# A hybrid decoder layer on one core: one pair of the second FFN computed plainly, and ScalarE and VectorE instructions placed by hand where stages change

## The chip, the cores and the metric

The kernel runs on one core of a Trainium2 chip. The core's engines work in parallel, each on its own queue of instructions: TensorE (matmuls and transposes; PE in the profile, its weight loads PEld), VectorE (DVE), ScalarE (ACT), GpSimd (POOL) and SyncE (SP), which here only starts DMA transfers. TensorE writes its products to PSUM, a memory of eight banks; everything else lies in SBUF. The metric is the time of the core in microseconds, the median of three runs: 1430.41 us before the change.

## The reference

A layer of a decoder is applied to 512 prompt tokens and to 64 sample tokens (8 sequences of 8), 576 in all, of width 1024, in fp32:

```python
x = x + 1/2 * swiglu(rmsnorm(x), ffn1)          # D_FF = 2816
P = rmsnorm(x) @ w_in                            # one combined projection
A = attention over 3 groups, (window, dilation) = (128,1), (512,4), (2048,16),
    4 heads x 64, RMSNorm of q and k; groups merged by their softmax denominators
B = gated linear attention, 4 heads, key 128, value 256, forget gate of rank 16;
    per-head RMSNorm, times silu(r_gate)
m = sigmoid(ga) * (A @ w_a_out) + sigmoid(gb) * (B @ w_b_out)
x = x + m @ w_out
x = x + 1/2 * swiglu(rmsnorm(x), ffn2)
swiglu(h) = (silu(h @ w_gate) * (h @ w_up)) @ w_down
```

Sample tokens attend to caches as well. Outputs are both groups of tokens, the new caches and the new states of the linear attention.

## The kernel before

**Tiles.** Activations are kept transposed: features on the 128 partitions, tokens along the columns, in two halves of 288. To reach fp32 accuracy each operand is split in two parts of the type fp32r, a high part that ScalarE rounds (line 138) and a low part that VectorE subtracts (line 139); each product then is three matmuls (high x high, high x low, low x high). A plain *group* is one 128-wide block of output features for one half of the tokens: 8 blocks of the contraction x 3 = 24 matmuls into one PSUM bank (`feat_mm`, lines 191 to 193). RMSNorm's gain is folded into the operand, and its factor per token, `row`, is multiplied to the product when VectorE takes it out of PSUM, so a stage may start before `row` is known.

**The FFN** (`sublayer`) has eleven pairs of 256 gate and up columns, worked off in phases of three pairs and a tail of two. The first `FIRST[g]` pairs are done plainly (class `First`, 8 groups of 24 matmuls for a pair; tiles pg). All later gates and ups are `Unit`s: seven products of block sums replace eight (12 matmuls for each product; tiles pX, pY, pZ), and so are the downs of the phases. Units need normalised operands in seven combinations, the tile `hop`, which VectorE and ScalarE build (`normal`, in steps `upper`, `lower`, `lower2`, `lower3`) during the plain groups, once `row` is there. `evac` takes a plain group out of PSUM: the factor (lines 642, 646, 648) and the Silu of the gate (643). `evacuate` calls it for groups that are at least two old, and then builds the pair's `second_operands`, the input of the down units. Before: three plain pairs in FFN 1 (g = 1), two in FFN 2 (g = 3). In FFN 2 the pool of weight tiles is exchanged at the seventh plain group (`buffers`).

**Between the stages.** When the last block of x is updated, `updated` puts off the sums of squares by `wait` groups and the row factors (`rows_`: transposes, and copies at line 222) by one more, so that TensorE runs the next stage's groups meanwhile; wait is 3 at the end of FFN 1 and 1 ahead of FFN 2.

**The mixer** (`mixer`) goes on after four r-gate groups that stand in the caller: their `gate_out` (oT = product x row, line 996), the r-gate's third block, then `PromptAttention` (head groups 1 and 2, then head group 0 with `steps0`, which runs beside the other r-gate blocks), `sample_steps` beside the first projections of the linear attention, the Silu of the eight r-gate tiles oT (line 1026), and the `Recurrence`.

**What sets the order.** TensorE's order is the order in which the program emits its instructions. The queues of the other engines are ordered by a scheduler, by readiness and by place in the emission; `keep_in_program_order` binds an instruction behind the one emitted just before it on its engine. `Weave` interleaves by hand: `run(main, between)` spreads the steps `between` evenly over the groups `main`, `put_off(n, step)` runs a step n groups later, and `loaded` gives a group a load that is emitted one group ahead. An empty step (`rest`) only takes a place. DMAs for weights are on SP's queue.

Of the kernel before, what the change touches and what calls it, by code (L numbers as in the profile page):

```python
# [18 lines left out]
P = 128  # L19
D = 1024  # L20
KD = D // P
SEQ = 512
# [12 lines left out]
GDV = 256  # L35
WCOLS = 1024
PAIRS = 3
FIRST = {1: 3, 3: 2}
AHEAD_W = 4


# [57 lines left out]
def hybrid_step_kernel(  # L99
# [131 lines left out]
    def updated(xT, m, h, g, sacc, sq, seen, wait=1):  # L231

        s = HALVES[h]
        operand(xT, m, s, g)
        if h not in [i for _, i in seen]:
            S.activation(sacc[:, s], xT[:, m, s], AF.Square)
        else:
            S.activation(sq, xT[:, m, s], AF.Square)
            V.tensor_add(sacc[:, s], sacc[:, s], sq)
        seen.append((m, h))  # L240
        if len(seen) < 2 * KD:
            return

        def sums():
            n = 5
            pr = ps_bg("pssq")
            V.memset(pr[NS:, 4:5], 0.0)
            for i in range(n):
                tok = sacc[:, SEQ:T] if i == 4 else sacc[:, i * P:(i + 1) * P]
                PE.matmul(pr[:tok.shape[1], i:i + 1], tok, ones, start=True, stop=True)  # L250
            rstd_of(rtok[:, :n], pr[:, :n], rms[:, :n], D)

        def rows_():
            spread([(rtok[:, t:t + 1], t * P) for t in range(4)], 0, SEQ)
            spread([(rtok[:NS, 4:5], SEQ)], SEQ, T)
            E.scaled(0, 1)

        weave.put_off(wait, sums)
        weave.put_off(wait + 1, rows_)

    E.scaled = lambda *halves: None
    wst = weights(4, 6, 1)
# [184 lines left out]
    def out(m, h):  # L447
        pt = ps_bg("py")
        for c in range(3):
            t0 = h * HALF + c * NC  # L450
            PE.transpose(pt[:NC, c * P:(c + 1) * P], xT[:, m, t0:t0 + NC], ident)
        y = ys2[:, (m + h) % 2]
        S.copy(y, pt[:NC, :3 * P])
        c = slice(m * P, (m + 1) * P)
        q = SP
        nt = 2 + (h == 0)
        q.dma_start(y_prompt[0, h * HALF:h * HALF + nt * NC, c].rearrange("(a p) c -> p a c", p=NC),
                    y[:, :nt * P].rearrange("p (a c) -> p a c", a=nt))
        if h:
            q.dma_start(y_prompt[0, SEQ - 32:SEQ, c], y[:32, 2 * P:])  # L460
# [88 lines left out]
def sublayer(E, xT, g, wg, wu, wd, wpre, after, nxt=lambda m: None, late=False, buffers=None):  # L549
# [41 lines left out]
    def normal():  # L591

        places.append(st.enter_context(E.sb("hop", 1, "right")).tile([P, 4 * slot], F32R, name="hop"))
        n = {}

        def factor(name, k, t):
            kk, s = {"A11": (k, 0), "A12": (k + 4, 0), "A21": (k, 1), "A22": (k + 4, 1)}[name]
            s = HALVES[s]
            V.scalar_tensor_tensor(t, xT[:, kk, s], E.gain[g][:, kk:kk + 1], E.row[:, s], op0=ALU.mult, op1=ALU.mult)
            n[name, k] = t  # L600
            return t

        def upper(name, k):
            E.split(*hact(name, k), factor(name, k, small("up", 8)))

        def lower(k):
            a21, a22 = (factor(x, k, small("s", 5)) for x in ("A21", "A22"))
            n["S1", k], n["S2", k] = small("s", 5), small("s", 5)
            V.tensor_add(n["S1", k], a21, a22)
            V.tensor_sub(n["S2", k], n["S1", k], n["A11", k])  # L610
            E.split(*hact("S2", k), n["S2", k])

        def lower2(k):
            E.split(*hact("S1", k), n["S1", k])
            V.tensor_sub(n["A11", k], n["A11", k], n["A21", k])
            E.split(*hact("S3", k), n["A11", k])

        def lower3(k):
            V.tensor_sub(n["A12", k], n["A12", k], n["S2", k])
            E.split(*hact("S4", k), n["A12", k])  # L620
            E.split(*hact("A22", k), n["A22", k])
# [15 lines left out]
    def evac(mat, f, h):  # L637
        s, po = HALVES[h], ps.pop((mat, f, h))[:, :HALF]
        c = kept.setdefault(f // 2, {})
        if mat == 0:  # L640
            c[C[f % 2, h]] = t = small("sg", 7) if f < 4 else small("up", 8)
            V.tensor_mul(t, po, E.row[:, s])
            S.activation(t, t, AF.Silu)
        else:
            u = small("s", 5)
            V.scalar_tensor_tensor(u, po, 0.5, E.row[:, s], op0=ALU.mult, op1=ALU.mult)
            t = c[C[f % 2, h]]
            V.tensor_mul(t, u, t)
            got[f // 2] = got.get(f // 2, 0) + 1

    got = {}

    def evacuate(i):
        for x in list(waiting):
# [50 lines left out]
    def up(pair):  # L705
        c = {}

        def done(i, x):
# [6 lines left out]
            if i == 6:  # L715
                c[name] = small("up", 8)
                V.scalar_tensor_tensor(c[name], x, 0.5, sg[name], op0=ALU.mult, op1=ALU.mult)
                kept[pair] = c
                if pair not in tail:
                    second_operands(pair)  # L720
                elif pair == tail[-1]:
                    last_operands()
                return
# [6 lines left out]
    def down(phase, m):  # L730
        f0, n = 2 * phase[0], len(phase)
        v = dv[:, f0:f0 + 2 * n, m * P:(m + 2) * P].rearrange("p (q two) c -> p two q c", two=2)

        def done(i, x):
            mm, h = {0: (0, 0), 1: (0, 0), 2: (1, 0), 3: (1, 1), 4: (1, 1), 5: (1, 0), 6: (0, 1)}[i]
            o = xT[:, m + mm, HALVES[h]]
            V.tensor_add(o, o, x)
        return Unit(E, [v[:, 0], v[:, 1]], lambda name, q: gact(name, phase[q]), n, done)


# [33 lines left out]

    final = []

    units = [fn(pair) for pair in phases[0][FIRST[g]:] for fn in (gate, up)]
    for n, phase in enumerate(phases):
        then = phases[n + 1] if n + 1 < len(phases) else tail
        units.append(gate(then[0]))  # L780
        downs = [down(phase, m) for m in range(0, KD, 2)]
        rest = [up(then[0])] + [fn(pair) for pair in then[1:] for fn in (gate, up)]
        units += rest + downs if then is tail else downs + rest
    lasts = [Last(m) for m in range(0, KD, 2)]

# [32 lines left out]

    for i, (_, u, n) in enumerate(slots):
        ahead(i)  # L820
        u.products(n)
        weave.tick()
        if isinstance(u, Last) and u.m == 4 and n in (1, 3):
            nxt(n // 2)
        evacuate(i)
        normal_steps(len(first) - i)
        if not any(isinstance(x[1], Unit) for x in slots[i + 1:]):
            for x in final:
# [158 lines left out]
def mixer(E, mxs, bk, xpool, opening):  # L987
# [7 lines left out]
    E.oT = oT = [E.slot(E.slotsA, F32, f"oT{m}") for m in range(KD)]  # L995
    gate_out = lambda m, s, ps: E.V.tensor_mul(oT[m][:, s], ps, E.row[:, s])

    for x in opening:
        gate_out(*x)
    weave.run(feat_groups(E, C_RG, [2], gate_out))  # L1000
    xpool.close()
    bk.close()
    bk = E.banks(4)
# [9 lines left out]
    weave.run(at.proj(0), at.steps12())  # L1013
    weave.run(feat_groups(E, C_RG, range(3, 8), gate_out), at.steps0())
    weave.finish()
    pst.close()
    bk.close()
    bk = E.banks(3)
# [1 line left out]
    hst = ExitStack()  # L1020
    gl = Recurrence(E, hst)
    early = gl.proj(0) + gl.proj(1)
    weave.run([lambda: gl.low_rank(Qm.pool)] + early[:13], sample_steps(E, sst, Qm))
    sst.close()
    for m in range(KD):
        S.activation(oT[m], oT[m], AF.Silu)
    gl.open(mxs)
    weave.run(early[13:], [gl.decay(0)])
    weave.run(gl.proj(2), gl.steps(0))
# [19 lines left out]
class PromptAttention:  # L1049
# [189 lines left out]
    def steps0(self):  # L1239
# [40 lines left out]

        rest = lambda: None
        (s0, t0, o0), (s1, t1, o1), (s2, t2, o2), (s3, t3, o3) = (one(n) for n in range(4))
        return [s0, s1, s2, t0, s3, t1, o0, t2, o1, t3, o2, rest, o3, rest, rest]


def sample_steps(E, st, Qm):
# [91 lines left out]
    def both(*steps):  # L1378
        def g():
# [2 lines left out]
        return g  # L1382

    f0(0)
    return [rest, k0[0], k0[1], s0[0], k0[2], s0[1], k0[3], both(s0[2], lambda: f0(1)), s0[3], rest, t0, rest,
            both(v0, lambda: f1(0)), o0, rest, rest, rest, k1[0], k1[1], s1[0], k1[2], s1[1], k1[3],
            both(s1[2], lambda: f1(1)), s1[3], rest, t1, rest, v1, rest, o1]


class Recurrence:  # L1390
# [18 lines left out]

    def low_rank(self, pool):  # L1410

        E, PE, S = self.E, self.E.PE, self.E.S
# [5 lines left out]
        S.copy(w[:, :, 0:16], raw)  # L1418
        E.V.tensor_sub(w[:, :, 16:32], raw, E.f32(w[:, :, 0:16]))
# [4 lines left out]
        for s in range(2):  # L1424
            S.copy(E.aup[32 * s:32 * s + 32], up)
        E.V.tensor_sub(E.aup[64:96], up, E.f32(E.aup[0:32]))
        self.lr = lr = hp.tile([96, T], F32R, tag="lr", name="lr", bufs=1)
        for s in HALVES:
# [311 lines left out]
```

## Time and profile before

| | |
|---|---|
| median of 3 runs | 1430.41 us (1430.05 to 1431.69) |
| the profiled execution | 1430.53 us, of which the span of the trace is 1428.7 |
| mean granted clock of TensorE | 0.993 |
| plain and unit weight splits on ScalarE (line 138) | 348 of 128x512, mean 577 ns; 115 of 128x1024, mean 971 ns |
| the same on VectorE (line 139) | 348, mean 632 ns; 115, mean 1128 ns |
| DMA | 144.28 MB, mean 101 GB/s |

"Busy" is time in which an engine executes; shares are of the span. The table of waits tells for how long TensorE stood before an instruction and who released it: `PE pf L191 <- ACT wh L138: 3.9, 1, 3.9` is TensorE ahead of the matmul of line 191 into tile pf, released by ScalarE's write of wh in line 138; sum of the waits, their number, the longest. In the tables of stretches and of the timeline, `xN` is the number of instructions. The granted clock is 1.00 where TensorE runs at full speed.

### The profile page before, as it was taken

What the parts mean: (1) busy time and instruction counts of PE and PEld (TensorE: products, weight loads), DVE (VectorE), ACT (ScalarE), POOL (GpSimd) and SP (SyncE); (2) the same over time, 40 slices, a digit from 0 to 9 for tenths busy, and PEclk for the clock granted to TensorE, in tenths of its full rate; (3) what the DMA queues carried; (4) which work ended last, traced back from release to release, by engine and by line L of the source; (5) the groups of instructions that cost most, each with busy time, mean ns of one, the idle gap of its engine ahead of it and who ended that gap; (6) DMA issues with size and microseconds to landing.
All of it is one profiled execution on the core that took longest, in us unless ns stands there. A gap on an engine that the chain in (4) does not pass through costs nothing.

```text
span 1428.7 us, 27553 instructions
## 1 busy us (share of the span) xinstructions
PE 1395.4 (98%) x10892; PEld 1366.0 (96%) x10892; DVE 1054.5 (74%) x2318; ACT 714.2 (50%) x1458; POOL 66.6 (5%) x105
## 2 busy tenths in 40 slices
PE   7999999999989999999999999999998999999997
PEld 7999999999989999898999999999998999999997
DVE  5999999998855454643576756455479999999882
ACT  7554564665444454632556634223345556466542
POOL 1000000000122211000000000000000000000000
PEclk9999999999999999999999999999999999999999
DMA  7313323332433432366223333335231333333332
GB/s 186 97 37 103 104 86 108 89 104 78 133 100 106 129 114 81 81 180 190 60 80 105 106 99 100 88 90 162 68 89 46 92 100 97 97 104 89 89 104 67
DMA packets 180688, 144.28 MB, mean 101 GB/s; under 512 B 7466, under 2 KB 179168, under 8 KB 180560
## 3 DMA queue, kind: packets, MB, share of 16 engines
q1 hardware_dynamic: 179456, 139.98, 33.8%
q0 software_dynamic: 1104, 2.54, 0.5%
q8 instruction: 86, 1.41, 0.4%
q14 instruction: 42, 0.34, 0.1%
HBM read 128.72 MB, written 13.78 MB: 100 GB/s over the span
## 4 chain that ended last, share of the span: by engine, by line
PE 89%; DVE 5%; ACT 2%; DMA 2%; issue 1%; SPq 1%; POOL 0%; ACTq 0%; POOLq 0%; DVEq 0%
PE pX L545 8%; PE pX L544 8%; PE pX L543 7%; PE pY L544 4%; PE pY L545 4%; PE pY L543 4%; PE pf L191 4%; PE pf L193 4%; PE pf L192 3%; PE ptok L956 3%; PE ptok L958 3%; PE ptok L957 3%; PE pZ L544 2%; PE pZ L545 2%; PE pZ L543 2%; PE pg L193 2%
## 5 line engine op out<-in xcount | busy, mean ns | idle before, releaser
L138 ACT CAST w<-raw 128x512 fp32r<-128x512 f32 (+1 forms) x348 | 196.8, 577 | 132.0 <-PE pX L545 31.2
L139 DVE TENSOR_TENSOR w<-raw,w 128x512 fp32r<-128x512 f32 (+1 forms) x348 | 215.9, 632 | 19.0 <-ACT w L138 17.4
L138 ACT CAST wh<-raw 128x1024 fp32r<-128x1024 f32 (+2 forms) x115 | 110.7, 971 | 118.1 <-PE pf L192 39.1
L139 DVE TENSOR_TENSOR wl<-raw,wh 128x1024 fp32r<-128x1024 f32 (+2 forms) x115 | 128.9, 1128 | 50.2 <-ACT wh L138 49.7
L545 PE MATMUL pX<-hop,w 128*128 128x288 f32 x544 | 161.5, 297 | 3.8 <-DVE w L139 3.8
L543 PE MATMUL pX<-hop,w 128*128 128x288 f32 x544 | 160.5, 295 | 1.1 <-ACT w L138 0.8
L544 PE MATMUL pX<-hop,w 128*128 128x288 f32 x544 | 161.4, 297 | 0.0
L191 PE MATMUL pf<-h,wh 128*128 128x288 f32 x384 | 119.9, 312 | 3.9 <-ACT wh L138 3.9
L956 PE MATMUL ptok<-wl,h 128*128 128x256 f32 x416 | 120.0, 289 | 0.0
L958 PE MATMUL ptok<-wh,h 128*128 128x256 f32 x416 | 116.9, 281 | 0.0
L957 PE MATMUL ptok<-wh,h 128*128 128x256 f32 x416 | 116.8, 281 | 0.0
L193 PE MATMUL pf<-h,wl 128*128 128x288 f32 x384 | 115.3, 300 | 0.4 <-DVE wl L139 0.4
L192 PE MATMUL pf<-h,wh 128*128 128x288 f32 x384 | 115.2, 300 | 0.0
L545 PEld LDWEIGHTS pX<-hop,w 128*128 128x128 f32 x544 | 102.9, 189 | 4.7 <-DVE w L139 4.7
L543 PEld LDWEIGHTS pX<-hop,w 128*128 128x128 f32 x544 | 103.1, 190 | 1.6 <-ACT w L138 1.0
L544 PEld LDWEIGHTS pX<-hop,w 128*128 128x128 f32 x544 | 103.0, 189 | 0.0
L191 PE MATMUL pg<-h,wh 128*128 128x288 f32 x320 | 96.4, 301 | 2.6 <-ACT wh L138 2.0
L193 PE MATMUL pg<-h,wl 128*128 128x288 f32 x320 | 95.6, 299 | 1.3 <-DVE wl L139 1.3
L192 PE MATMUL pg<-h,wh 128*128 128x288 f32 x320 | 95.7, 299 | 0.0
L191 PEld LDWEIGHTS pf<-h,wh 128*128 128x128 f32 x384 | 74.4, 194 | 7.0 <-ACT wh L138 4.1
L544 PE MATMUL pY<-hop,w 128*128 128x288 f32 x272 | 80.4, 296 | 0.0
L545 PE MATMUL pY<-hop,w 128*128 128x288 f32 x272 | 80.3, 295 | 0.0
(428 smaller groups left out, 4257.6 us busy)
## 6 DMA issues: line engine op xcount, KB each, us to landing
raw<-in_w_in_dram SPq DMA_DIRECT2D x58, 512.0 KB, 3.9
raw<-in_ffn_gate_dram SPq DMA_DIRECT2D x45, 512.0 KB, 3.8
raw<-in_ffn_up_dram SPq DMA_DIRECT2D x44, 512.0 KB, 3.8
raw<-in_ffn_down_dram SPq DMA_DIRECT2D x48, 384.0 KB, 3.3
raw<-in_ffn_down_dram SPq DMA_DIRECT2D x8, 512.0 KB, 3.5
kv<-in_cache_swa_kv_dram SPq DMA_DIRECT2D x32, 128.0 KB, 4.2
kv<-in_cache_swa_kv_dram SPq DMA_DIRECT2D x16, 256.0 KB, 4.4
S<-in_state_gla_dram SPq DMA_DIRECT2D x4, 1024.0 KB, 6.6
```

The costliest lines, as they stand in the source:

```text
L138: S.copy(hi, src)
L139: V.tensor_sub(lo, src, f32(hi))
L191: PE.matmul(ps, h, ah, start=first and j == 0, stop=False)
L192: PE.matmul(ps, h, al, start=False, stop=False)
L193: PE.matmul(ps, l, ah, start=False, stop=last and j == n - 1)
L543: PE.matmul(ps, wh[:, k], ah, start=opens and k == 0, stop=False, skip_group_check=True)
L544: PE.matmul(ps, wh[:, k], al, start=False, stop=False, skip_group_check=True)
L545: PE.matmul(ps, wl[:, k], ah, start=False, stop=k == self.nk - 1, skip_group_check=True)
L956: PE.matmul(po[:, :256], ah, wl, start=(k == 0), stop=False)
L957: PE.matmul(po[:, :256], al, wh, start=False, stop=False)
L958: PE.matmul(po[:, :256], ah, wh, start=False, stop=(k == KD - 1))
```

## The change

The change has these parts, in the order of the program.

1. FFN 2 has three plain pairs.
2. The row factors are put off by `wait + 2` groups instead of `wait + 1` where wait is above 1, so after FFN 1 only.
3. Of the last block of output columns, one of the DMAs of y_prompt is started by ScalarE.
4. The splits for `hop`, and in FFN 2 all of `evac`, are bound to emission order. In FFN 2 nothing is evacuated ahead of slot 6; at slot 6 `evacuate` stands ahead of the slot's products.
5. In both FFNs the up unit of pair 3 is emitted ahead of the downs of the first phase, and pair 3's second operands are built only at the last product of these downs.
6. In the mixer the r-gate's third block runs ahead of the row multiplications of the first four groups.
7. The eight Silus of oT move from behind the sample attention to its opening, in emission order.
8. The low-rank projection of the forget gate becomes two groups with a load ahead, behind six of the linear attention's groups; its DMAs, on SP and POOL, are emitted at its old place.
9. `steps0` has its two last rests at the front; `sample_steps` has four more rests and one less, 33 steps in place of 31.

The diff, without lines that only reindent:

```diff
-FIRST = {1: 3, 3: 2}
+FIRST = {1: 3, 3: 3}
...
-        weave.put_off(wait + 1, rows_)
+        weave.put_off(wait + (2 if wait > 1 else 1), rows_)
...
-            q.dma_start(y_prompt[0, SEQ - 32:SEQ, c], y[:32, 2 * P:])
+            (S if m == KD - 1 else q).dma_start(y_prompt[0, SEQ - 32:SEQ, c], y[:32, 2 * P:])
...
+        def parts(hi, lo, src):
+            keep(S.copy(hi, src))
+            keep(V.tensor_sub(lo, src, E.f32(hi)))
...
-            V.tensor_mul(t, po, E.row[:, s])
-            S.activation(t, t, AF.Silu)
+            keep(V.tensor_mul(t, po, E.row[:, s]))
+            keep(S.activation(t, t, AF.Silu))
...
+    keep = E.tc.keep_in_program_order if buffers else lambda ins: ins
...
+                if pair in hold:
+                    return
                 if pair not in tail:
                     second_operands(pair)
...
             V.tensor_add(o, o, x)
+            if (m, i) == (KD - 2, 6) and phase is phases[0]:
+                for pair in hold:
+                    second_operands(pair)
...
+    hold = phases[1][:1] if FIRST[g] == PAIRS else ()
...
+        if n == 0 and hold:
+            downs, rest = rest[:1] + downs, rest[1:]
...
         ahead(i)
+        if buffers and i == 6:
+            evacuate(i)
         u.products(n)
...
-        evacuate(i)
+        if not buffers or i > 6:
+            evacuate(i)
...
+    weave.run(feat_groups(E, C_RG, [2], lambda *x: opening.append(x)))
     for x in opening:
         gate_out(*x)
-    weave.run(feat_groups(E, C_RG, [2], gate_out))
...
     weave.finish()
+    for m in range(KD):
+        E.tc.keep_in_program_order(S.activation(oT[m], oT[m], AF.Silu))
...
-    weave.run([lambda: gl.low_rank(Qm.pool)] + early[:13], sample_steps(E, sst, Qm))
+    between = sample_steps(E, sst, Qm)
+    low = gl.low_rank(Qm.pool)
+    weave.run(early[:6] + low + early[6:13], between)
     sst.close()
-    for m in range(KD):
-        S.activation(oT[m], oT[m], AF.Silu)
...
-        return [s0, s1, s2, t0, s3, t1, o0, t2, o1, t3, o2, rest, o3, rest, rest]
+        return [rest, rest, s0, s1, s2, t0, s3, t1, o0, t2, o1, t3, o2, rest, o3]
...
-    return [rest, k0[0], k0[1], s0[0], k0[2], s0[1], k0[3], both(s0[2], lambda: f0(1)), s0[3], rest, t0, rest,
-            both(v0, lambda: f1(0)), o0, rest, rest, rest, k1[0], k1[1], s1[0], k1[2], s1[1], k1[3],
-            both(s1[2], lambda: f1(1)), s1[3], rest, t1, rest, v1, rest, o1]
+    return [rest, k0[0], k0[1], s0[0], k0[2], s0[1], k0[3], both(s0[2], lambda: f0(1)), s0[3], rest, rest, t0, rest,
+            both(v0, lambda: f1(0)), rest, o0, rest, rest, k1[0], k1[1], s1[0], k1[2], s1[1], k1[3],
+            both(s1[2], lambda: f1(1)), s1[3], rest, rest, t1, rest, v1, rest, o1]
...
-        E.SP.dma_start(raw, wv[:, :, C_LR:C_LR + 16])
+        keep(E.SP.dma_start(raw, wv[:, :, C_LR:C_LR + 16]))
...
-            E.G.dma_start(up[16 * s:16 * s + 16], E.g_alpha_up)
+            keep(E.G.dma_start(up[16 * s:16 * s + 16], E.g_alpha_up))
...
+        return [loaded(lambda: first and first.pop()(), group, s) for s in HALVES]
```

More of the change, by code (lines that the diff above doesn't have):

```diff
@@ L601, in factor @@
             return t
+        def parts(hi, lo, src):
+            keep(S.copy(hi, src))
+            keep(V.tensor_sub(lo, src, E.f32(hi)))
         def upper(name, k):
-            E.split(*hact(name, k), factor(name, k, small("up", 8)))
+            parts(*hact(name, k), factor(name, k, small("up", 8)))
         def lower(k):
@@ L610, in lower @@
             V.tensor_sub(n["S2", k], n["S1", k], n["A11", k])
-            E.split(*hact("S2", k), n["S2", k])
+            parts(*hact("S2", k), n["S2", k])
         def lower2(k):
-            E.split(*hact("S1", k), n["S1", k])
+            parts(*hact("S1", k), n["S1", k])
             V.tensor_sub(n["A11", k], n["A11", k], n["A21", k])
-            E.split(*hact("S3", k), n["A11", k])
+            parts(*hact("S3", k), n["A11", k])
         def lower3(k):
             V.tensor_sub(n["A12", k], n["A12", k], n["S2", k])
-            E.split(*hact("S4", k), n["A12", k])
-            E.split(*hact("A22", k), n["A22", k])
+            parts(*hact("S4", k), n["A12", k])
+            parts(*hact("A22", k), n["A22", k])
         normed.extend((upper, name, k) for name in ("A11", "A12") for k in range(4))
@@ L641, in evac @@
             c[C[f % 2, h]] = t = small("sg", 7) if f < 4 else small("up", 8)
-            V.tensor_mul(t, po, E.row[:, s])
-            S.activation(t, t, AF.Silu)
+            keep(V.tensor_mul(t, po, E.row[:, s]))
+            keep(S.activation(t, t, AF.Silu))
         else:
             u = small("s", 5)
-            V.scalar_tensor_tensor(u, po, 0.5, E.row[:, s], op0=ALU.mult, op1=ALU.mult)
+            keep(V.scalar_tensor_tensor(u, po, 0.5, E.row[:, s], op0=ALU.mult, op1=ALU.mult))
             t = c[C[f % 2, h]]
-            V.tensor_mul(t, u, t)
+            keep(V.tensor_mul(t, u, t))
             got[f // 2] = got.get(f // 2, 0) + 1
     got = {}
+    keep = E.tc.keep_in_program_order if buffers else lambda ins: ins
     def evacuate(i):
@@ L1410, in low_rank @@
     def low_rank(self, pool):
-        E, PE, S = self.E, self.E.PE, self.E.S
+        E, PE, S, keep = self.E, self.E.PE, self.E.S, self.E.tc.keep_in_program_order
         hp = self.hp
@@ L1416, in low_rank, with load, group @@
         w = pool.tile([P, KD, 32], F32R, tag="lw2", name="lw2", bufs=1)
-        E.SP.dma_start(raw, wv[:, :, C_LR:C_LR + 16])
-        S.copy(w[:, :, 0:16], raw)
-        E.V.tensor_sub(w[:, :, 16:32], raw, E.f32(w[:, :, 0:16]))
+        keep(E.SP.dma_start(raw, wv[:, :, C_LR:C_LR + 16]))
         up = pool.tile([32, 4 * GDK], F32, tag="up", name="up", bufs=1)
         for s in range(2):
-            E.G.dma_start(up[16 * s:16 * s + 16], E.g_alpha_up)
[L1424 to L1428, printed above, removed]
+            keep(E.G.dma_start(up[16 * s:16 * s + 16], E.g_alpha_up))
+        def load():
+            keep(S.copy(w[:, :, 0:16], raw))
+            E.V.tensor_sub(w[:, :, 16:32], raw, E.f32(w[:, :, 0:16]))
+            for s in range(2):
+                keep(S.copy(E.aup[32 * s:32 * s + 32], up))
+            E.V.tensor_sub(E.aup[64:96], up, E.f32(E.aup[0:32]))
+        first = [load]
+        def group(s):
+            if not hasattr(self, "lr"):
+                self.lr = hp.tile([96, T], F32R, tag="lr", name="lr", bufs=1)
+            lr = self.lr
             po = E.ps_acc("plr")
```

## The prediction

> **What bounds the kernel now.** I read the page first.
>
> ```profile
> span 1428.7 us, 27553 instructions
> PE 1395.4 (98%) x10892; PEld 1366.0 (96%) x10892; DVE 1054.5 (74%) x2318; ACT 714.2 (50%) x1458; POOL 66.6 (5%) x105
> ...
> PE 89%; DVE 5%; ACT 2%; DMA 2%; issue 1%; SPq 1%; POOL 0%; ACTq 0%; POOLq 0%; DVEq 0%
> ```
>
> TensorE is busy for 98% of the span and carries 89% of the chain. Whatever does not stop it or add to it is worth nothing. So the next view is the list of whom TensorE waited for, of which I keep the lines that a stage change owns:
>
> ```profile
> PE pX L545 <- DVE w L139: 4.3, 3, 3.5
> PE pf L191 <- ACT wh L138: 3.9, 1, 3.9
> ...
> PE psS L1160 <- DVE st L1164: 2.0, 1, 2.0
> PE pg L191 <- ACT wh L138: 2.0, 1, 2.0
> ...
> PE pg L193 <- DVE wl L139: 1.3, 2, 0.7
> PE ptP L1346 <- DVE Ps L1340: 1.3, 1, 1.3
> ...
> PE pX L543 <- ACT w L138: 0.8, 1, 0.8
> ...
> PE ptOs L1368 <- DVE osam L1363: 0.6, 1, 0.6
> PE pf L193 <- DVE wl L139: 0.4, 1, 0.4
> PE pX L543 <- ACT sg L694: 0.3, 1, 0.3
> ```
>
> Each is a single event, some 16 us in all. The third view is the table of stretches, for the rate of matmuls and the granted clock behind the long waits (columns: stretch, its length, busy time and count of PE, PEld, DVE, ACT, POOL, clock, DMA share, GB/s):
>
> ```profile
> 56.00:76.00 20.00, 20.00 (x153) 20.00 (x152) 19.57 (x46) 10.11 (x21) 0.00 (x0) 1.00 0.34 99
> ...
> 417.86:421.27 3.41, 1.32 (x4) 0.97 (x5) 1.75 (x2) 2.58 (x4) 0.00 (x0) 0.50 0.00 0
> 421.27:424.69 3.42, 3.42 (x16) 3.42 (x16) 0.62 (x1) 0.21 (x1) 0.00 (x0) 0.50 0.79 225
> ...
> 581.70:585.11 3.41, 3.37 (x19) 3.04 (x20) 3.19 (x21) 3.04 (x12) 0.00 (x0) 0.50 0.01 2
> 585.11:588.53 3.42, 3.42 (x16) 3.42 (x15) 2.62 (x16) 3.40 (x12) 0.00 (x0) 0.50 0.00 0
> ...
> 1093.70:1097.10 3.40, 3.21 (x12) 2.90 (x12) 3.37 (x8) 2.34 (x6) 0.00 (x0) 0.50 0.00 0
> ```
>
> 153 plain matmuls take 20.00 us, 0.131 each. Behind three of the waits the clock is 0.50 for one or two stretches of 3.41 us, and 16 matmuls fill 3.42 us, 0.21 to 0.24 each. A long wait is thus paid twice.
>
> **The change part by part.** The profiled execution took 1430.53 us (span 1428.7, the rest around it); the median of the three runs is 1430.41, 0.1 less.
>
> *Opening of the mixer.* The chain of waits there reads:
>
> ```profile
> 414.06 0.13 PE pf L193
> ...
> 415.47 0.59 ACT row L222
> ...
> 416.46 0.82 DVE oT L996 x2
> 417.30 1.26 ACT oT L1026 x2
> 418.56 0.94 ACT wh L138
> 419.52 1.24 DVE wl L139
> ...
> 421.65 0.24 PE pf L192
> ```
>
> The cast of the r-gate's third weight stands on ScalarE's queue behind the row copies and two Silus of oT that the scheduler pulled up from L1026. The change emits those weights ahead of the row factors, puts the row transposes one group later (wait 3 now gives +2) and pins all Silus elsewhere. Then the cast runs before the row copy, and TensorE has two more groups (48 x 0.131 = 6.3 us) to cover row copies (0.59) and the output multiplications. The waits of 3.9 and 0.4 go; so does the slow clock: 20 matmuls from 419.5, when the quoted cast ends (418.56 + 0.94), to 424.69, less 0.4 of wait, took 4.8 us instead of 20 x 0.131 = 2.6. Gain 4.3 + 2.1 = 6.4. Late next is a PSUM bank for the first token group: the last oT multiplication (0.82 for two, 0.4 each) follows the last group. I take 0.2 for it. **-6.2.**
>
> *Prompt attention.* The steps of head group 0 begin two steps later.
>
> ```profile
> 577.18 3.74 DMA N<-scr
> 581.74 2.68 PE psS L1160 x16
> ...
> 590.10 1.09 PE psS L1160 x16
> ```
>
> The second scores wait for banks that free only once N is read back, near 581. With 15 steps over 10 groups the two rests move the first scores behind the second group, near 577.7, and the second behind the third, past 582, with N landed. The wait of 2.0 goes, and the slow clock: 2.68 - 1.09 = 1.6 on these scores, and from 584.4 to 588.5 at 0.24 instead of 0.131 another 4.1 x (1 - 0.131/0.24) = 1.9. **-5.5.** The last output step now stands behind the last group without rests; its two ScalarE/VectorE splits are covered by the next stage's first matmuls, which need no such bank.
> The Trainium skill (TensorE: Matmul & The Clock Gate, Why this matters for your kernels) warns only of TensorE gaps above about 3 us. By that this wait would cost 2.0, and the sum would come out 3.5 us higher. The trace does not agree: the clock is 0.50 from 581.70, right behind a gap of 2.0.
>
> *Sample attention.* Two rests more let a group pass between scores and transposes and between sums and output: waits 1.3 and 0.6 go. But 33 steps over 15 groups put the first half's transposes and sums behind the same sixth group, so the sums wait for ScalarE's copy of the transposes:
>
> ```profile
> 640.10 1.28 ACT L1338 ACT_TABLE_LOAD   x1
> ...
> 649.38 0.59 ACT L1347 COPY PTs<-ptP 128x512 f32<-128x512 f32 x1 [1.00 <-PE ptP L1346]
> ```
>
> That is 0.59 less the fifth transpose and its sums: 0.4, up to 1.6 with a weight cast (0.94 in the chain above) in front. The eight Silus now stand together on ScalarE at the opening: 8 x 0.63 (two took 1.26) and one table load of 1.28, 6.3 us. Behind them are queued the casts of later weights (three pairs are split already) and the key copies, which TensorE needs after two groups and some transposes, near 8 us: 0 to 1 of waiting, I take 0.5. Two of the old Silu detours (a table load there and back amid the exponentials) vanish; no TensorE wait hung on them. The low-rank loads, pinned on SP and POOL behind the cache loads, are needed only after six groups (about 20 us): nothing. **-1.9 + 0.9 = -1.0.**
>
> *Opening of FFN 2.*
>
> ```profile
> 1047.90 0.47 DVE sg L642
> ...
> 1048.74 1.04 ACT wh L138
> ...
> 1026.00:1046.00 20.00, 20.00 (x153) 19.73 (x152) 11.10 (x28) 7.57 (x17) 1.18 (x1) 1.00 0.28 79
> 1046.00:1066.00 20.00, 17.31 (x129) 16.84 (x128) 13.78 (x28) 8.53 (x15) 0.00 (x0) 1.00 0.35 106
> ```
>
> The seventh group waits 2.0 + 0.7: its weights' cast stood behind a Silu that waited for VectorE's evacuation of the sixth. Now nothing is evacuated before the seventh group, and what is, is pinned behind the splits of the seventh's and ninth's weights. The wait goes if those splits run while TensorE is in groups four to six. **-2.7**; between -2.7 and +3.3 (first rival).
>
> *A third plain pair in FFN 2.* Plain, pair 2 is 8 groups x 24 = 192 matmuls; as two seven-product units 2 x 7 x 12 = 168. 24 x 0.131 = **+3.1**, all on the path. Its VectorE work shrinks, and the normalised operands are spread over 24 groups instead of 16. The wait for the hop weights, 3.5 + 0.3, and the slow clock behind it (12 matmuls in 3.2 us instead of 1.6) are 5.4 together. FFN 1 already runs three plain pairs; its own change shows what should remain:
>
> ```profile
> PE pX L545 <- DVE w L139: 0.8, 2, 0.5
> ```
>
> With the 0.8 of `pX L543` in the first list, which lies there too, 1.6 us, in three pieces, without a slower clock. So **-3.8** (between 0 and -5.4).
>
> *The unit order* (up of pair 3 ahead of the down products, its second operands held) is in both FFNs. VectorE's work ahead of the first late product, the second operands of pairs 1 and 2, is as before, and it was that which FFN 1's 1.6 us waited for. I take 0, from -1.6 to +1.6.
>
> *Tail.* One output DMA of the last column goes to ScalarE's queue:
>
> ```profile
> 1424.21 0.45 SPq L460 DMA_DIRECT2D out_dram<-sacc  x1
> ...
> 1425.32 0.53 SPq L457 DMA_DIRECT2D out_dram<-sacc  x1
> ```
>
> SP's last issue comes 0.45 earlier. **-0.4.**
>
> Sum: -6.2 - 5.5 - 1.0 - 2.7 + 3.1 - 3.8 - 0.4 = -16.5; 1430.5 - 16.5 = **1414.0**. Its own bounds: the unit order's and the hop's +-1.6, the sample stage's +1.9, about 1410 to 1419.
>
> **The rivals.**
>
> *FFN 2 keeps its stops* (0.15). The ninth group's split needs a weight tile. If that tile lies over one that the sixth group still reads, the chain is cast 1.04, subtraction 1.24, evacuation 0.47 after the sixth group: 2.8 us instead of 2.7, and being in one piece it may take the clock to 0.50 for up to two stretches, 3.41 x (1 - 0.131/0.24) = 1.5 each. VectorE would also start its backlog later, and the hop wait would stay: 2.8 + 3.0 + 3.8 more, 1423.6. For it: VectorE's and ScalarE's pinned queues have nothing else to run there. Against: of 20 us in the first stretch VectorE is busy for 11, so there is room, and the splits' raw weights come early.
>
> *ScalarE's block of Silus stops TensorE* (0.10). If the key copies and a cast fall behind all 6.3 us, the first sample scores wait about 2 us, and the clock may follow as at 581.7: 2 + 3.4 more, 1419.4.
>
> *Pins without effect* (0.07). A pin binds an instruction only to the one traced just before it; the scheduler may still pull others up. If the waits of the opening and of FFN 2 return, 6.2 + 2.7 + 3.8 are lost: 1426.7.
>
> *VectorE becomes the bound in FFN 2* (0.08), the slower side. In FFN 1's plain groups VectorE is busy 19.57 of 20. In FFN 2 it may not evacuate for the first 20 us, then owes the same work in the other 55, each split waiting for a cast (1.04 x 9), each evacuation for a Silu. What it lacks at the hop, TensorE waits. Work that FFN 1 spreads over 60 us (59) in 55 gives 4, the casts 9; to cancel the gain and pass the bound it must reach 16.5 + 2.9 = 19.4, that is 0.3 us lost at each of 19 evacuations. Then 1433.4 and more. Against: the evacuations are emitted a group behind, with six banks of slack.
>
> **How the numbers follow.** The forecast has 0.60, the rivals 0.15, 0.10, 0.07 and 0.08. The likeliest case gives 1414.0. Most unseen costs are new waits, so the range reaches up: from 1409 to 1425 it takes in all but the last two, about 0.85. A measurement of this kernel can tell about 0.2%, 2.9 us. Faster by more: 0.89, the forecast and the first three rivals less 0.03 for a pin rival that costs somewhat more; within: that 0.03; slower: 0.08.
>
> **What would show it.** In the changed profile: no wait of `pf L191` on ACT wh near 415, no clock of 0.50 inside the span but at its end, no `psS L1160` wait; ACT Silu of oT as one block of eight with one table load; 24 more matmuls (10916); `pg L191` without a wait in FFN 2; `pX L545` waits of below 1 us each at both hops. The forecast is wrong if the total of TensorE's waits stays above some 12 us, if a clock of 0.50 stands anywhere between 400 and 1400, or if VectorE is busy without a break ahead of FFN 2's first late product.

## The result and the profile after

The changed kernel takes 1414.03 us, the median of four runs (1412.59 to 1414.53), against 1431.05 before (1430.05 to 1434.33; the three runs ahead of the prediction and one more): a ratio of 0.9876 with a 95% interval of 0.9857 to 0.9894. The forecast was 1414.0. The profiled execution took 1414.37.

The lines of its page that answer to those of before:

```profile
span 1412.5 us, 27578 instructions
PE 1392.0 (99%) x10916; PEld 1363.9 (97%) x10916; DVE 1048.4 (74%) x2302; ACT 706.6 (50%) x1440; POOL 66.6 (5%) x105
...
PE 93%; DVE 3%; ACT 2%; DMA 1%; SPq 1%; issue 1%; POOL 0%; ACTq 0%; POOLq 0%; DVEq 0%
```

TensorE has 24 matmuls more (10916 for 10892), as the third plain pair must give, and the span is 16.2 shorter all the same. Whom it waited for, the longest of the list:

```profile
PE ptr L321 <- DMA xtok<-in_x_prompt_dram: 5.1, 1, 5.1
PE ptr L321 <- ACT xT L324: 2.0, 1, 2.0
PE pX L545 <- DVE w L139: 1.4, 2, 0.7
PE pT L1200 <- DVE R L1184: 1.1, 1, 1.1
PE psOs L1380 <- ACT PTs L1367: 0.9, 1, 0.9
...
PE ptok L974 <- DVE oT L1014: 0.6, 1, 0.6
...
PE psOs L1376 <- DVE PTn L1371: 0.4, 1, 0.4
```

`pf L191` (3.9 before), `psS` (2.0), `pg L191` and `L193` (2.0 + 0.7), `ptP` (1.3), `ptOs` (0.6) and the 3.5 of `pX L545` are gone. New are two waits of the sample attention's sums (psOs) and one of a token group (ptok).

The two traces, cut at the first matmul of each stage, say where the 16.2 came from:

| stage (from, before / after) | before | after | difference | forecast |
|---|---|---|---|---|
| start and FFN 1 (0) | 400.93 | 401.68 | +0.75 | 0 |
| mixer opening, r-gate groups (400.93 / 401.68) | 27.83 | 21.89 | -5.94 | -6.2 |
| projections, prompt attention (428.76 / 423.57) | 194.97 | 189.54 | -5.43 | -5.5 |
| sample attention (623.73 / 613.11) | 68.19 | 67.93 | -0.26 | -1.0 |
| recurrence to w_out (691.92 / 681.04) | 334.61 | 336.13 | +1.52 | 0 |
| FFN 2 (1026.53 / 1017.17) | 395.36 | 389.04 | -6.32 | -3.4 |
| after the last matmul (1421.89 / 1406.21) | 6.76 | 6.26 | -0.50 | -0.4 |

The sum was met closer than its terms: FFN 2 gave 2.9 more than forecast, and the start, the sample attention and the recurrence gave back 3.0. (A *late product* is one of the units', behind the plain groups.) The start differs as much from profile to profile: over all profiles FFN 1's first late product comes at 93.7 to 96.2. The recurrence, which the change doesn't touch, has this (stretches; columns as in the prediction):

```profile
735.37:738.78 3.41, 3.41 (x29) 2.76 (x30) 2.48 (x4) 0.00 (x0) 0.00 (x0) 1.00 0.53 137
738.78:742.20 3.42, 3.42 (x17) 2.97 (x16) 0.35 (x2) 1.05 (x4) 0.00 (x0) 0.50 1.10 345
```

TensorE waits for nothing here, yet the clock is 0.50 for one stretch, 1.5 us. This is looked at below.

### The profile page after: what moved, and what is told of

It is laid out like the page before. It is cut to its first block, busy times and chain, and to the rows that moved or that the text cites. A ratio compares the mean times of both kernels' runs of the same rounds, so it can differ in the third digit from the quotient of the medians.

```text
span 1412.5 us, 27578 instructions
## 1 busy us (share of the span) xinstructions
PE 1392.0 (99%) x10916; PEld 1363.9 (97%) x10916; DVE 1048.4 (74%) x2302; ACT 706.6 (50%) x1440; POOL 66.6 (5%) x105
## 3 DMA queue, kind: packets, MB, share of 16 engines
q8 instruction: 86, 1.41, 0.4%
## 4 chain that ended last, share of the span: by engine, by line
PE 93%; DVE 3%; ACT 2%; DMA 1%; SPq 1%; issue 1%; POOL 0%; ACTq 0%; POOLq 0%; DVEq 0%
PE pX L545 7%; PE pX L544 7%; PE pX L543 7%; PE pf L191 4%; PE pY L544 4%; PE pY L545 4%; PE pY L543 4%; PE pf L192 4%; PE pf L193 4%; PE ptok L974 3%; PE ptok L976 3%; PE ptok L975 3%; PE pg L191 3%; PE pg L193 3%; PE pg L192 3%; PE pZ L544 2%
## 5 line engine op out<-in xcount | busy, mean ns | idle before, releaser
L138 ACT CAST w<-raw 128x512 fp32r<-128x512 f32 (+1 forms) x336 | 190.2, 575 | 124.9 <-PE pX L545 37.8
L139 DVE TENSOR_TENSOR w<-raw,w 128x512 fp32r<-128x512 f32 (+1 forms) x336 | 208.5, 632 | 19.6 <-ACT w L138 17.0
L138 ACT CAST wh<-raw 128x1024 fp32r<-128x1024 f32 (+2 forms) x119 | 115.2, 975 | 137.4 <-PE pf L192 41.3
L139 DVE TENSOR_TENSOR wl<-raw,wh 128x1024 fp32r<-128x1024 f32 (+2 forms) x119 | 133.9, 1132 | 55.0 <-ACT wh L138 54.6
L545 PE MATMUL pX<-hop,w 128*128 128x288 f32 x512 | 151.3, 295 | 1.4 <-DVE w L139 1.4
L544 PE MATMUL pX<-hop,w 128*128 128x288 f32 x512 | 151.4, 296 | 0.0
L543 PE MATMUL pX<-hop,w 128*128 128x288 f32 x512 | 150.5, 294 | 0.4 <-ACT w L138 0.4
L974 PE MATMUL ptok<-wl,h 128*128 128x256 f32 x416 | 120.1, 289 | 0.6 <-DVE oT L1014 0.6
L191 PE MATMUL pf<-h,wh 128*128 128x288 f32 x384 | 118.5, 309 | 0.0
L191 PE MATMUL pg<-h,wh 128*128 128x288 f32 x384 | 115.2, 300 | 0.7 <-ACT h L228 0.7
L193 PE MATMUL pg<-h,wl 128*128 128x288 f32 x384 | 114.5, 298 | 0.6 <-DVE wl L139 0.6
L192 PE MATMUL pg<-h,wh 128*128 128x288 f32 x384 | 114.8, 299 | 0.0
L193 PE MATMUL pf<-h,wl 128*128 128x288 f32 x384 | 113.9, 296 | 0.0
L545 PEld LDWEIGHTS pX<-hop,w 128*128 128x128 f32 x512 | 96.4, 188 | 1.9 <-DVE w L139 1.9
L543 PEld LDWEIGHTS pX<-hop,w 128*128 128x128 f32 x512 | 96.5, 188 | 0.6 <-ACT w L138 0.6
L544 PEld LDWEIGHTS pX<-hop,w 128*128 128x128 f32 x512 | 96.5, 188 | 0.0
L974 PEld LDWEIGHTS ptok<-wl,h 128*128 128x128 f32 x416 | 78.6, 189 | 2.7 <-issue 1.3
L975 PEld LDWEIGHTS ptok<-wh,h 128*128 128x128 f32 x416 | 78.6, 189 | 0.0
L976 PEld LDWEIGHTS ptok<-wh,h 128*128 128x128 f32 x416 | 78.4, 189 | 0.0
```

Source lines behind the costliest of these rows:

```text
L138: S.copy(hi, src)
L139: V.tensor_sub(lo, src, f32(hi))
L191: PE.matmul(ps, h, ah, start=first and j == 0, stop=False)
L192: PE.matmul(ps, h, al, start=False, stop=False)
L193: PE.matmul(ps, l, ah, start=False, stop=last and j == n - 1)
L543: PE.matmul(ps, wh[:, k], ah, start=opens and k == 0, stop=False, skip_group_check=True)
```

## The experiments

### FFN 2: the third pair or the order

**Two plain pairs in the changed kernel.**

```diff
-FIRST = {1: 3, 3: 3}
+FIRST = {1: 3, 3: 2}
```

> The changed kernel with two plain pairs in FFN 2 again; all else of the change stays. Theory (room): the wait ahead of FFN 2's first late product went because VectorE has 24 plain groups instead of 16 to build the normalised operands in. Then 24 matmuls go (-3.1) and the wait of about 3.5 with the slow clock behind it comes back (+5.4): about 1416.3 us, 2.3 above the changed kernel, with VectorE busy without a break ahead of the wait. Rival (order): the later evacuation and the fixed order alone took the wait away; then only the 24 matmuls go and it is 3.1 below the changed kernel, about 1411. Second rival: VectorE, which evacuates nothing for six groups, is later than before and the wait is above 5 us: 1418 or more.

With two pairs `hold` is empty in FFN 2, so the unit order of part 5 goes there with the third pair; the next run has the pair without that order.

Measured: 1419.26 us, ratio to before 0.9916 (0.9899 to 0.9933), 5.2 above the changed kernel. Its waits at the first late products, and VectorE ahead of them:

```profile
PE pX L545 <- DVE w L139: 3.1, 1, 3.1
PE pX L543 <- ACT sg L700: 2.1, 1, 2.1
```

```profile
1035.00:1055.00 20.00, 20.00 (x153) 20.00 (x152) 16.27 (x39) 11.73 (x23) 0.00 (x0) 1.00 0.24 72
1055.00:1069.00 14.00, 14.00 (x108) 14.00 (x107) 14.00 (x35) 6.51 (x18) 0.00 (x0) 1.00 0.14 39
```

VectorE is busy for 14.00 of 14.00 us and still late: two waits, 5.2 in all, and three stretches at 0.50 behind them. The second rival holds: with two pairs and the change's evacuation VectorE is later than in the kernel before (5.2 of waits against 3.5 + 0.3).

**Three plain pairs in the kernel before.** The same line the other way round.

> The kernel before with three plain pairs in FFN 2 and nothing else of the change (the place of the up unit of pair 3 and its second operands are as before). Theory (room): the wait at the first late product falls to below 1.6 us without a slow clock, the wait of the seventh group (2.0 + 0.7) stays: -5.4 + 3.1, and up to +1.6 of what is left, 1428 to 1430. Rival (order): without the fixed order the wait stays at 3.5 with its slow clock, and the time is 3.1 above before, 1433.5.

Measured: 1428.03 us, ratio 0.9977 (0.9965 to 0.9988). All waits of FFN 2 up to its late products:

```profile
PE pg L191 <- ACT wh L138: 2.0, 1, 2.0
PE pg L193 <- DVE wl L139: 0.7, 1, 0.7
```

The wait at the late products is not below 1.6 but absent. The third pair does it alone, with nothing of the new order, and it does it by room for VectorE. Of the kernel before and then of this one, the last stretch ahead of the first late product (1082.7 and 1109.1):

```profile
1066.00:1082.00 16.00, 16.00 (x123) 16.00 (x122) 16.00 (x41) 8.43 (x19) 0.00 (x0) 1.00 0.12 34
```

```profile
1085.90:1109.00 23.10, 23.10 (x177) 23.10 (x176) 17.94 (x41) 10.20 (x23) 0.00 (x0) 1.00 0.13 40
```

VectorE, the third engine of the line, is busy for 16.00 of 16.00 in the one and for 17.94 of 23.10 in the other.

**Evacuation at every slot, the order bound.**

```diff
-        if buffers and i == 6:
-            evacuate(i)
         u.products(n)
...
-        if not buffers or i > 6:
-            evacuate(i)
+        evacuate(i)
```

> The changed kernel, but FFN 2 evacuates at every slot as the kernel before did, behind the slot's products; the instructions stay bound to emission order. Theory: the seventh group waits again for its weights, since their cast stands behind a Silu that waits for VectorE's evacuation: 2 to 2.7 above the changed kernel, about 1416.5. Rival: the fixed order alone keeps the splits ahead; then no wait and 1414.

Measured: 1413.98 us, ratio 0.9877 (0.9859 to 0.9895), and no wait of pg in FFN 2. FFN 2 takes 389.4 from its first to its last matmul, 389.0 with the late evacuation. The rival holds: the bound order frees the seventh group without the late evacuation.

**Nothing bound to emission order.**

```diff
-    keep = E.tc.keep_in_program_order if buffers else lambda ins: ins
+    keep = lambda ins: ins
...
-        E.tc.keep_in_program_order(S.activation(oT[m], oT[m], AF.Silu))
+        S.activation(oT[m], oT[m], AF.Silu)
...
-        E, PE, S, keep = self.E, self.E.PE, self.E.S, self.E.tc.keep_in_program_order
+        E, PE, S, keep = self.E, self.E.PE, self.E.S, lambda ins: ins
```

> The changed kernel with every instruction freed that the change binds to emission order (the splits for hop and the evacuations of FFN 2, the eight Silus, the loads of the low-rank projection); their places in the program stay. Theory: the places do the work, as the scheduler goes by emission where operands are ready; no wait comes back and it is 1414. Rival: the scheduler pulls Silus of oT up again to the mixer's opening and to the sample attention, and evacuations ahead of splits in FFN 2; the waits of the seventh group (2.7) and a part of the opening's 3.9 come back, with a slow clock behind the latter: 1417 to 1423.

Measured: 1416.33 us, ratio 0.9898 (0.9876 to 0.992). Of the changed kernel and then of this one, the eight Silus (a line's instructions: durations in ns, first and last start):

```profile
L1035 ACT ACTIVATE oT<-oT x8: 667/668/687, 614.9 to 618.9; 128x576 f32<-128x576 f32 x8
L1035 ACT ACT_TABLE_LOAD  x1: 1283/1283/1283, 613.6 to 613.6; - x1
```

```profile
L1035 ACT ACTIVATE oT<-oT x8: 669/684/686, 421.1 to 610.5; 128x576 f32<-128x576 f32 x8
L1035 ACT ACT_TABLE_LOAD  x3: 1283/1283/1283, 572.2 to 592.9; - x3
```

And this one's waits from the sample attention to FFN 2's late products:

```profile
PE pg L191 <- ACT wh L138: 2.0, 1, 2.0
PE pg L193 <- DVE wl L139: 0.7, 1, 0.7
PE psOs L1376 <- DVE PTn L1371: 0.4, 1, 0.4
```

Freed, the Silus scatter over 190 us with three table loads, and no TensorE wait comes of it. What comes back is FFN 2's 2.7, to the tenth, though the late evacuation is still there. With the run before, that this wait went is the bound order's doing. The opening keeps its gain without any binding. And the sums' wait of 0.9 (`psOs L1380`) is gone: the low-rank copies were pulled up to 409.

### The mixer's opening

**Row factors one group earlier.**

```diff
-        weave.put_off(wait + (2 if wait > 1 else 1), rows_)
+        weave.put_off(wait + 1, rows_)
```

> The changed kernel with the row factors put off by one group less after FFN 1 (wait + 1 as before). The row copies are then emitted ahead of the r-gate's third weights. Theory: on ScalarE the casts of these weights (two of 0.94) stand behind the row copies, which wait for TensorE's transposes; about 1.6 of the old wait of 3.9 comes back, without a slow clock: 1415.6 us. Rival: the third block's place ahead of the row multiplications does all, since the raw weights land long before: 1414.

Measured: 1415.34 us, ratio 0.9895 (0.988 to 0.991), 1.3 above the changed kernel. The casts stand behind the row copies again (timeline of ScalarE):

```profile
414.94 0.70 ACT L222 COPY row<-prow 128x512 f32<-128x512 f32 x2 [12.07 <-PE prow L221]
415.53 2.00 ACT L138 CAST wh<-raw 128x1024 fp32r<-128x1024 f32 x2
```

Against the expectation, the profile has a slow clock as well: 0.50 for two stretches from 417.46.

**The kernel before with the Silus moved and bound, nothing else.**

```diff
     weave.finish()
+    for m in range(KD):
+        E.tc.keep_in_program_order(S.activation(oT[m], oT[m], AF.Silu))
...
-    for m in range(KD):
-        S.activation(oT[m], oT[m], AF.Silu)
```

> The kernel before, with only the eight Silus of oT moved to the sample attention's opening and bound there. Theory (Silus in the way): in the mixer's opening the cast of the r-gate's third weight runs right behind the row copies, 2.3 us earlier; the wait of 3.9 falls to 1.6 and the slow clock behind it (2.1) goes: 1426.0. Rival (row copies in the way): the cast was held by the row copies and the multiplications anyway, and the time stays within 1 of 1430.4. Second rival: the block stops TensorE at the sample attention, above 1431.

Measured: 1428.05 us, ratio 0.9976 (0.9964 to 0.9988). Both kernels have the same two waits in the opening:

```profile
PE pf L191 <- ACT wh L138: 1.5, 1, 1.5
PE pf L193 <- DVE wl L139: 1.1, 1, 1.1
```

Without the Silus the first wait falls from 3.9 to 1.5 and no slow clock follows, as expected, but the second wait grows from 0.4 to 1.1: VectorE's subtraction of 1.2 now shows. So 1.7 of the opening's 4.3 are the two Silus, and 2.6 the row copies, which the extra group puts behind the casts. (The same two waits come with a slow clock in one profile and without it in the other; the opening takes 26.78 there and 24.13 here.) In the changed kernel TensorE begins the third block at 415.5, and ScalarE has cast its weights some 10 us earlier (timeline of ScalarE):

```profile
404.05 1.99 ACT L138 CAST wh<-raw 128x1024 fp32r<-128x1024 f32 x2
419.38 1.05 ACT L138 CAST wh<-raw 128x1024 fp32r<-128x1024 f32 x1 [13.34 <-PE prow L221]
420.33 0.69 ACT L222 COPY row<-prow 128x512 f32<-128x512 f32 x2
```

### The prompt attention and the slow clock

**The old list of steps0 in the changed kernel.** The two rests go back to the end.

> The changed kernel with the old list of steps0, no rests in front. Theory: the third scores wait 2.0 again for a bank that frees once N has landed, and the clock is 0.50 for up to two stretches behind it: 5.5 above the changed kernel, 1419.5. Rival (only the wait counts, the slow clock came of something else): 2.0 above, 1416.0. Second rival: N lands earlier in the changed order and nothing comes back: 1414.

Measured: 1418.49 us, ratio 0.9914 (0.9897 to 0.9931), 4.5 above the changed kernel. The waits there, and the stretches of 3.41 us that hold the first:

```profile
PE psS L1180 <- DVE st L1184: 2.0, 1, 2.0
...
PE ptk L1334 <- DMA kv<-in_cache_swa_kv_dram: 0.5, 1, 0.5
```

```profile
572.37:575.78 3.41, 1.70 (x13) 1.47 (x12) 0.38 (x3) 0.00 (x0) 0.00 (x0) 1.00 0.70 184
575.78:579.20 3.42, 2.98 (x26) 2.67 (x27) 3.20 (x21) 2.78 (x11) 0.00 (x0) 1.00 0.01 3
```

The wait of 2.0 is back, and a cache read that comes 0.5 late besides. But in this profile no slow clock follows. The same idle time cost two slow stretches in the kernel before, one in the kernel before with three plain pairs, and none in the kernel before with the Silus moved (a wait of 1.9) and here. The wait alone does not make up the 4.5: projections and prompt attention are 3.3 longer than in the changed kernel, as the two sets of 16 scores behind the wait take 1.77 and 1.57 at a clock of 1.00 where 1.09 was reckoned, and the sample attention is 0.9 longer.

**Needless matmuls ahead of the wait, in the kernel before.** The second r-gate group of that stage starts with nine products that its own first product then overwrites.

```diff
+        if c0 == C_RG and (m, h) == (3, 1):
+            E.feat_mm(po[:, :HALF], ws[m], 0, P, E.hH, E.hL, range(3), HALVES[h])
         E.feat_mm(po[:, :HALF], ws[m], 0, P, E.hH, E.hL, range(KD), HALVES[h])
```

> The kernel before with nine needless matmuls (1.2 us of TensorE): one r-gate group ahead of the wait of 2.0 in the prompt attention starts with nine of its products, which are then overwritten. Theory (the clock falls where TensorE was busy for too small a share of a stretch of 3.41 us): the wait shrinks to 0.9, TensorE's share in that stretch rises from 0.41 to 0.75, the clock stays at 1.00 and the kernel is faster by 1.6 + 1.9 = 3.5 although it does more: about 1427. Rival (the slow clock comes of the score matmuls, whatever the wait): the nine matmuls only fill the wait and the time stays at 1430.5.

Measured: 1433.39 us, ratio 1.0009 (0.9994 to 1.0024). The waits of the stage:

```profile
PE psS L1162 <- DVE st L1166: 0.7, 1, 0.7
PE psS L1162 <- DVE st L1267: 0.6, 1, 0.6
PE psS L1162 <- DVE st L1265: 0.5, 1, 0.5
```

In the profile the wait fell to 0.7, no slow clock followed, and from the first scores to the end of the stage it is 105.75 us instead of 107.20, with 1.2 us more of matmuls. But two new waits took 1.1 of the gain, and over the runs none is left: the forecast of the time failed. The same stage without the filler shows a reason. It takes 107.20 with two slow stretches (before), 105.94 with one (three plain pairs) and 104.75 with none (the Silus moved). The filler costs its 1.2 each time; what it is to avert does not come each time.

### Where the slow clock comes from

All slow stretches inside the span last 3.41 us or twice that, and what lies between two of them is a whole multiple (before, 424.69 to 581.70: 46 times 3.413). They are thus cut from a grid, which lies elsewhere against the program in each profile. Cut on its own grid up to the last matmul, the fourteen traces hold 17 stretches at a clock of 1.00 in which PE was busy for less than 0.49: behind all 17 the clock is 0.50. Of the 150 that were busy for 0.49 to 0.95, one is followed by it (0.55). So what a wait of 2.0 does depends on how the grid cuts it. Of the kernel before, the stretch that holds the wait ahead of the slow clock at 581.70:

```profile
578.29:581.70 3.41, 1.41 (x11) 1.18 (x9) 0.65 (x5) 0.00 (x0) 0.00 (x0) 1.00 0.58 166
```

PE is busy for 1.41 of 3.41 there, 0.41; with the old list of steps0 above it was 1.70, 0.50. The two openings with the same waits part in the same way: 0.47 and 0.55. (These shares were read off the traces of the runs; none was made to test them.)

The recurrence has a case of another kind. Its first step is 16 matmuls of 128 and 32 columns (32 in the trace) and takes 3.8 us from its first to its last start, once for each of four heads, without a wait. Twelve profiles (before, after, and those of all experiments but the two that cut this step) hold 48 such steps. In 8 a whole stretch of the 3.41 us grid, read off from where the clock changes, lies inside the step, and behind 6 of these the clock is 0.50. Where less of a stretch lies inside, 40 steps, it never is. In the two whole stretches without it, the stretch begins 0.09 and 0.12 behind the step's first matmul, in the six 0.19 to 0.61; what this means is open. One of the six, in the kernel that evacuates at every slot:

```profile
775.02:778.43 3.41, 3.41 (x30) 2.72 (x29) 2.48 (x4) 0.00 (x0) 0.00 (x0) 1.00 0.44 116
778.43:781.84 3.41, 3.41 (x16) 2.96 (x16) 0.57 (x2) 1.05 (x4) 0.00 (x0) 0.50 1.10 346
```

PE counts as busy for all of the first stretch, so it is not idle time alone that lowers the clock. Of the 5508 stretches that were busy for 0.95 or more, these six are the only ones with a slow clock behind them.

**The step cut in two halves, with a group between.**

```diff
-        def weights():
-            pd, pc = ps_bg("pdiag"), ps_bg("pcross")
-            for sc in range(4):
+        def weights(half):
+            if half == 0:
+                t.pd, t.pc = ps_bg("pdiag"), ps_bg("pcross")
+            pd, pc = t.pd, t.pc
+            for sc in range(2 * half, 2 * half + 2):
...
+            if half == 0:
+                return
...
-        return [weights, turn_keys, *nxt, f(states, 0)
+        gap = [] if nxt else [lambda: None]
+        return [f(weights, 0), turn_keys, *gap, f(weights, 1), *nxt, f(states, 0)
```

> The changed kernel with the recurrence's first step (16 matmuls of 128 and 32 columns in a row, 3.8 us) cut in two halves with a projection group between. Theory (in the profiles so far a clock of 0.50 follows wherever a stretch of the fixed 3.41 us grid lies wholly inside this step, 8 such slow stretches in ten profiles, 1.5 us each): no slow clock in the recurrence any more, 1.2 below the changed kernel, 1412.8, with less spread. Rival: the clock falls there for another reason and falls on; or the later second half lets the outputs wait: 1414 or above.

Measured: 1412.33 us (1411.69 to 1413.24), ratio 0.9861 (0.9842 to 0.9881), 1.7 below the changed kernel. Its profile has no slow clock from the start to the last matmul. One profile says little, as that of FFN 1's bound order below, with the step uncut, has none either. The runs say more: the mean granted clock is 0.999 in all five, and in all four of the last kernel below, which has the cut too; of the runs of the changed kernel and of the next two kernels, without the cut, 3 of 14 do. In time the direction fits the theory; the two intervals overlap.

### The rests

**The first half's sums a group later.**

```diff
-    ... rest, rest, t0, rest, both(v0, lambda: f1(0)), rest, o0, rest, rest, k1[0], ...
+    ... rest, rest, t0, rest, rest, both(v0, lambda: f1(0)), rest, o0, rest, k1[0], ...
```

> The changed kernel with one rest of sample_steps moved: the first half's sums come a group after its transposes. Theory: the two waits of the sums (0.38 and 0.89, behind the low-rank copies on ScalarE) go, nothing takes their place: 1.3 below the changed kernel, 1412.7. Rival: the sums, now later, hold the caches' buffers longer, so that the second half's keys come late and the wait goes there: 1414.

Measured: 1414.08 us (1412.54 to 1415.99), ratio 0.9874 (0.9853 to 0.9895): no gain that can be told, the rival's number. Both waits are gone, and the only one left in the sample attention is not the rival's but one for the low-rank weights:

```profile
PE plr L1458 <- DVE lw L1444: 0.6, 1, 0.6
```

**FFN 1 bound to emission order too.**

```diff
-    keep = E.tc.keep_in_program_order if buffers else lambda ins: ins
+    keep = E.tc.keep_in_program_order
```

> The changed kernel with the splits for hop and the evacuations bound to emission order in FFN 1 too. Theory: in FFN 1 the three waits of 1.8 at the first late products come of VectorE, busy without a break; order can't change its sum of work, so 1413 to 1415. Rival (order): they go as FFN 2's went, 1412.2. Second rival: VectorE and ScalarE wait for each other in the fixed order and the wait grows by 3 or more, 1417.

Measured: 1413.67 us, ratio 0.9872 (0.9849 to 0.9894), as the theory had it. The waits at FFN 1's late products are 2.6 instead of 1.8; order gives nothing there:

```profile
PE pX L545 <- DVE w L139: 2.2, 2, 1.5
PE pX L543 <- ACT w L138: 0.4, 1, 0.4
```

"Busy without a break" holds for VectorE from 82.8 on in the changed kernel, 20 us ahead of the first of these waits at 102.7; in the 5 us before that it stands idle for 3.4.

**The cut step, the later sums, and the low-rank groups behind seven groups instead of six.**

```diff
-    weave.run(early[:6] + low + early[6:13], between)
+    weave.run(early[:7] + low + early[7:13], between)
```

> The changed kernel with the recurrence's first step cut in two, the first half's sums of the sample attention a group later and the low-rank groups one group later. Theory: no slow clock in the recurrence (1.2 to 1.7 less, as measured with the cut alone) and no wait of the sums (1.3 less), with 0.6 of wait ahead of the low-rank matmuls gone as well: 1411.2 us. Rival: the sums' wait only moves to another place of the sample attention, as it did with the later sums alone: 1412.3.

Measured: 1411.14 us (1409.97 to 1411.6), ratio 0.9858 (0.9842 to 0.9875), 2.9 below the changed kernel by the medians and the fastest kernel of this case, though its interval overlaps that of the changed kernel. No wait is left in the sample attention, and no slow clock in the span but at its end.

## Why the prediction was right, point by point

- *Opening, -6.2: right (-5.94).* Casts ahead of the row copies, two groups as cover. The slow clock in the term, 2.1, was there in all three profiles with the old opening (before, three plain pairs, filler). The bank wait is 0.6 (`ptok L974`) where 0.2 was taken, since a weight split of 1.2 stands on VectorE ahead of the oT multiplications.
- *Prompt attention, -5.5: the wait is right, the slow clock was a draw, and so was the close hit.* The stage gave 5.43 in this pair of profiles. But 3.5 of the term were two slow stretches of one profile, taken as certain; of the four profiles with the old list and no filler they stand in one, one stretch in another, none in two. Some of the 3.5 was not the clock either: the scores behind the wait take 1.77 at a clock of 1.00. The old list costs 4.5 over its runs, 0.9 of it, by its profile, in the sample attention.
- *Sample attention, -1.0: too much by 0.7.* The waits of 1.3 and 0.6 went. The sums wait 1.3 instead of the 0.4 taken, within the bound of 1.6, though not for a weight cast: the low-rank copies, bound to this place, stand ahead of the copy (timeline of ScalarE):

```profile
638.75 0.29 ACT L1443 CAST lw<-lw 128x128 fp32r<-128x128 f32 x1
638.94 1.25 ACT L1447 CAST aup<-up 32x512 fp32r<-32x512 f32 x2
640.22 0.58 ACT L1367 COPY PTs<-ptP 128x512 f32<-128x512 f32 x1
```

  "Nothing" for the low-rank projection was therefore wrong. The block of Silus, taken at 0.5, delayed nobody. By the waits the stage should have gained 0.6; 0.3 stays open.
- *Opening of FFN 2, -2.7: right in size by the waits; of the two reasons given only the second counts.* The bound order does it without the late evacuation, and the late evacuation does not without the bound order.
- *Third plain pair and hop wait, +3.1 - 3.8: this is the term that was mis-sized.* FFN 1's rest of 1.6 was carried over, and FFN 2 has none. In FFN 2 VectorE has slack nearly to the first late product at 1095.6; in FFN 1 of the same profile it has none from 82.8 on, and its first late product comes at 95.3:

```profile
1017.00:1037.00 20.00, 20.00 (x152) 19.73 (x151) 9.97 (x21) 5.73 (x11) 1.18 (x1) 1.00 0.42 117
...
1077.00:1096.00 19.00, 19.00 (x146) 19.00 (x144) 17.51 (x40) 9.82 (x23) 0.00 (x0) 1.00 0.17 51
```

```profile
82.78:103.00 20.22, 19.57 (x148) 19.34 (x147) 20.18 (x50) 11.93 (x29) 0.00 (x0) 1.00 0.10 27
```

  The 19.57 of 20 that the prediction read in FFN 1 stands at 56 to 76 of the kernel before; from 76 to 96 the share there is 16.53 of 20. So it is not the share that parts the two FFNs, but where VectorE's last idle time ends: 3.0 ahead of the first late product in FFN 2 (1092.6), 12.5 ahead in FFN 1. That makes 1.6 of the 2.9 by which FFN 2 did better. The rest is that the two stops of before were sized too low: from start to start of the matmuls, what exceeds 0.131 each is 3.2 more than after around the seventh group (2.7 was taken) and 6.3 more around the late products (5.4 was taken).
- *Unit order, 0; tail, -0.4: right.* FFN 1's waits went from 1.6 to 1.8; in FFN 2 the order was not tried by itself, as no wait was left to it. The tail gave 0.5; its DMA was not tried by itself either.
- *The rivals.* FFN 2's stops went, and no wait stands behind the block of Silus, so the first two did not come. "VectorE becomes the bound" showed, far smaller than priced, with two plain pairs only, and "pins without effect" is refuted for FFN 2.
- *What would show it wrong.* Two of the three signs were set badly. The waits add up to 14.2, above the 12 named, because 7.1 of them are the start's, which nothing here could change. And a clock of 0.50 does stand between 400 and 1400, for a reason that the prediction had not seen.

## What to carry to other kernels

Before choosing between an edit that reorders an engine's work and one that gives it room, see whether that engine is busy without a break ahead of the wait: here 24 more matmuls of TensorE removed a wait that the new evacuation order alone, with two pairs, made longer. A bound order pays where an instruction that could run stands behind one that waits, and it costs where it fixes a copy ahead of one that is needed sooner. A slow stretch seen in one profile is a chance, not a cost: price it over several profiles, or see whether the wait can leave TensorE idle for half of one stretch of the grid.

## What the hardware showed beyond that

The clock of TensorE is decided on a grid of 3.41 us that keeps its own time: in the fourteen profiles its first boundary lies anywhere from 0.2 to 2.9 us behind the program's first instruction. The Trainium skill (TensorE: Matmul & The Clock Gate, Part 1: The HAM clock gate) says the same, a free-running window of 3413 ns, and the traces agree. Behind every stretch of this grid in which TensorE was busy for less than 0.49, 17 in all, the clock was 0.50; a wait of 2.0 was therefore followed by two, one or no slow stretches. And a step of small matmuls without any wait lowered the clock in 6 of the 8 cases in which a whole stretch lay inside it, at 1.5 us for each slow stretch. This is likely a part of what spreads the times of one kernel over some 2 us.
